# RWKV chunk products on 64x64 quarters of the array, gram matrices by 64-row halves, in a one-core Trainium2 decoder block

## The chip, the cores and the metric

One core of a Trainium2 chip runs one launch of a hybrid decoder block. The metric is the device time of a launch in microseconds. The kernel before takes 2877.19 us (median of 3 runs, 2877.06 to 2877.37).

The core has five engines, each with an instruction queue of its own that it works through in order: PE (TensorE, matmuls, with the loading of weights recorded apart as PEld), DVE (VectorE), ACT (ScalarE), POOL (GpSimd) and SP (which only issues transfers here). They wait for one another through semaphores.

## The reference

Input x is 512 tokens of 2048 channels. The block computes a fused projection of the normalised input, RWKV-7 time mixing (16 heads of 64), sliding-window attention, gated merging, and a gated convolutional FFN. The change lies in the time mixing alone:

```python
def step(state, inp):
    r_t, k_t, v_t, w_t, ka_t, kb_t = inp
    sa = jnp.einsum('bhvk,bhk->bhv', state, ka_t)
    state = (state * w_t[:, :, None, :] + sa[..., None] * kb_t[:, :, None, :]
             + v_t[..., None] * k_t[:, :, None, :])
    y = jnp.einsum('bhvk,bhk->bhv', state, r_t)
    return state, y
...
_, y = lax.scan(step, state0, xs)          # over 512 tokens, per head
mu = jnp.mean(y, axis=-1, keepdims=True)
var = jnp.mean(jnp.square(y - mu), axis=-1, keepdims=True)
y = ((y - mu) * lax.rsqrt(var + GN_EPS)).reshape(B, S, RW_DIM)
```

## The kernel before, in words

The scan is computed in 8 chunks of 64 tokens (`NCH`, `C`). Two heads are worked on together as a pair, head 0 on partitions 0 to 63 and head 1 on 64 to 127 (`HV`); there are 8 pairs. A pair goes through three functions. `early(p)` projects k, r and v and makes decays and keys. `late(p)` makes, for every chunk:

- the gram products (L700): `BKK` (keys times inverse decay, 128 columns: own head's b, other kind's k) against `BAR` (a and r of both heads, 256 columns), masked by DVE into `BX`, `OA`, `MD`, `MO` (L704). A 128x128 result holds a 64x64 block for each head and two blocks that belong to no head, masked to zero, so that a product over 128 rows serves both heads.
- the inverse of a triangular matrix by doubling: `tt`, `X`, `AI`, `BT` are set up (L708 to L720, with transposes of `BX` at L713), then five levels (`LEVELS[1:]`) of two f16 products each, `mm3(AI, ..)` and `mm3(BT, ..)` (L761, L762).
- the bulk products of all chunks: `GV` and `KV` (L724, from `OA` and `KO` with `VV`, the centred v).
- the chain over chunks: `psG` (L802) to `G` on DVE, `psU` (L808) to `UU` on ACT, `psS` (L815) to `SS` on DVE, and so to the next chunk.
- the output products y of a chunk: `MO` with `VV`, `MD` with `UU`, `BAR` with `SS` (L821, L822, L824), added up in one PSUM tile, copied to `yt`.

`final(p)` normalises `yt` into `yd`, transposes it (L843) and applies the gate (L609). After each pair three gate tiles of the big projection are computed (`emit_gate`). The calls go `late(p)`, `early(p + 1)`, `final(p)`, gates.

The projections in `early` and in the gates are three matmuls per 128 rows of weights, in a split-float form (L260 to L262, 512 columns). Their weights come by transfer as `raw`, and ACT and DVE split them into `whi` (L243) and `wlo` (L244), 12 matmuls for each split, 4 buffers deep. 288 of these matmuls fall between one pair's first gram product and the next pair's.

A scheduler at build time sets the order on each engine from its own estimates; `pin` ties an instruction behind the one traced before it on its engine. The order is then fixed. PSUM tiles named `bulk` come from a ring of 3 banks. `OA`, `KO` and `yd` share one buffer (tag "ko"), `GV` and `yt` another.

Of the kernel before, what the change touches and what calls it, by code (L numbers as in the profile page):

```python
# [8 lines left out]
F32 = mybir.dt.float32  # L9
# [125 lines left out]
def block_kernel(ctx: ExitStack, tc: tile.TileContext, d: Dims, a: dict, out: bass.AP):  # L135
# [145 lines left out]
    if True:  # L281
# [243 lines left out]
        with ExitStack() as pr:  # L525
# [142 lines left out]
            def late(p, st):  # L668
# [24 lines left out]

                BKE = wk.tile([P, NCH, P], F32, name="BKE", tag="BKE")
                dve.tensor_tensor(BKE, BKK, ee.unsqueeze(2).to_broadcast([P, NCH, P]), op=ALU.mult)
                OA = wk.tile([P, NCH, P], F32, name="OA", tag="ko")
                for n0 in range(0, NCH, 2):
                    ps = bulk()
                    for j in range(2):
                        pe.matmul(ps[:, j * 4 * C : (j + 1) * 4 * C], BKK[:, n0 + j],  # L700
                                  BAR[:, n0 + j].rearrange("p a h c -> p (a h c)"), start=True, stop=True)
                    pq = ps.rearrange("p (n a c) -> p n a c", n=2, a=2)
                    for t, a, nm in ((BX, 0, "own"), (OA, 0, "other"), (MD, 1, "own"), (MO, 1, "other")):
                        dve.tensor_tensor(t[:, n0 : n0 + 2], pq[:, :, a], mb(nm, 2)[:, :, a * P : (a + 1) * P], op=ALU.mult)  # L704
                for g in range(2):
                    ns = slice(g * HN, (g + 1) * HN)
                    for h, (lo, hi) in enumerate(HV):
                        dve.tensor_tensor(tt[lo:hi, ns], BX[lo:hi, ns, lo:hi], mb("m1", HN, (lo, hi)), op=ALU.mult)  # L708
                    dve.tensor_tensor(tt[:, ns], tt[:, ns], mb("istack", HN), op=ALU.add)
                    split(X[:, 0, ns], X[:, 1, ns], tt[:, ns])  # L710
                    ps = bulk().rearrange("p (n c) -> p n c", c=P)
                    for j in range(HN):
                        pe.transpose(ps[:, j], BX[:, g * HN + j], ident)  # L713
                    at_ = wk.tile([P, HN, P], F32, name="at_", tag="at_")
                    dve.scalar_tensor_tensor(at_, ps, SG, mb("idsg", HN), op0=ALU.mult, op1=ALU.add)
                    split(AI[:, 0, ns], AI[:, 1, ns], at_)
                    act.activation(BX[0:C, ns, 0:C], tt[0:C, ns], AF.Copy, scale=1.0 / SG)
                    dve.tensor_scalar(BX[C:P, ns, C:P], tt[C:P, ns], 1.0 / SG, None, op0=ALU.mult)
                    for i in range(2):
                        dve.tensor_tensor(BT[:, i, ns], AI[:, i, ns], mb("t1bd", HN), op=ALU.mult)  # L720
                def bulk_mm(dst, l, r):
                    ps = bulk()
                    for n in range(NCH):
                        pe.matmul(r3(ps)[:, n], l(n), r(n), start=True, stop=True)  # L724
                    act.activation(dst, r3(ps), AF.Copy)

                ps = bulk()
                for t in range(NT):
                    ts = slice(t * P, (t + 1) * P)
# [2 lines left out]
                dve.reduce_sum(vm, r3(ps), axis=AX.X)  # L732
                dve.tensor_scalar(vm, vm, -1.0 / HD, None, op0=ALU.mult)
                for a, (fl, fh) in enumerate(HV):
                    for h in range(2):
                        ol, oh = HV[1 - h]
                        dve.tensor_tensor(VV[ol:oh, a::2], r3(ps)[fl:fh, h::2],
                                          vm[fl:fh, h::2].unsqueeze(2).to_broadcast([C, NT, C]), op=ALU.add)
                GV = wk.tile([P, NCH, C], F32, name="GV", tag="yt")
                bulk_mm(GV, lambda n: OA[:, n], lambda n: VV[:, n])  # L740
                for g in range(2):
                    ns = slice(g * HN, (g + 1) * HN)
                    ps = bulk().rearrange("p (n c) -> p n c", c=P)
                    for j in range(HN):
                        pe.transpose(ps[:, j], BKE[:, g * HN + j], ident)
                    if g == 0:
                        KO = wk.tile([P, NCH, P], F32, name="KO", tag="ko")
                        pool.memset(KO[0:C, :, 0:C], 0.0)
                        pool.memset(KO[C:P, :, C:P], 0.0)
                    for h, (lo, hi) in enumerate(HV):  # L750
                        ol, oh = HV[1 - h]
                        act.activation(KD[lo:hi, ns, lo:hi], ps[lo:hi, :, lo:hi], AF.Copy)
                        act.activation(KO[lo:hi, ns, ol:oh], ps[lo:hi, :, ol:oh], AF.Copy)
# [45 lines left out]
                for n in range(NCH):  # L799
                    if n:  # L800
                        ps = chn.tile([P, C], F32, name="psG", tag="chn")
                        pe.matmul(ps, BAR[:, n, 0].rearrange("p h c -> p (h c)"), SS[:, n], start=True, stop=True)  # L802
                        G = wk.tile([P, C], F32, name="G", tag="G", bufs=2)
                        dve.tensor_tensor(G, GV[:, n], ps, op=ALU.add)
                    else:
                        G = GV[:, 0]
                    ps = chn.tile([P, C], F32, name="psU", tag="chn")
                    pe.matmul(ps, BX[:, n], G, start=True, stop=True)  # L808
                    act.activation(UU[:, n], ps, AF.Copy)
# [6 lines left out]
                    dve.tensor_tensor(SS[:, n + 1], KV[:, n], ps, op=ALU.add)  # L816

                ps = bulk()
                for n in range(NCH):
                    dst = r3(ps)[:, n]  # L820
                    pe.matmul(dst, MO[:, n], VV[:, n], start=True, stop=False)  # L821
                    pe.matmul(dst, MD[:, n], UU[:, n], start=False, stop=n == 0)  # L822
                    if n:
                        pe.matmul(dst, BAR[:, n, 1].rearrange("p h c -> p (h c)"), SS[:, n], start=False, stop=True)  # L824
                yt = wk.tile([P, NCH, C], F32, name="yt", tag="yt")
                act.activation(yt, r3(ps), AF.Copy)
                return ag, bon, yt

            def final(p, st):
                ag, bon, yt = st  # L830
                sq = wk.tile([P, NCH, C], F32, name="gn", tag="gn")
                act.activation(sq, yt, AF.Square)
                ss = wk.tile([P, NCH], F32, name="ssy", tag="ssy")
                dve.reduce_sum(ss, sq, axis=AX.X)
                rs = rsqrt_small(wk, ss, 1.0 / HD, GN_EPS)
                yd = wk.tile([P, NT, 2, C], F32, name="yd", tag="ko")
                for a, (al, ah) in enumerate(HV):
                    for h, (lo, hi) in enumerate(HV):
                        dve.tensor_tensor(yd[al:ah, :, h], yt[lo:hi, a::2],
                                          rs[lo:hi, a::2].unsqueeze(2).to_broadcast([C, NT, C]), op=ALU.mult)  # L840
                ps = bulk()
                for t in range(NT):
                    pe.transpose(ps[:, t * P : (t + 1) * P], yd[:, t].rearrange("p h c -> p (h c)"), ident)  # L843
# [607 lines left out]
```

## Time and profile before

| | |
|---|---|
| median of 3 runs | 2877.19 us |
| the profiled execution | 2876.5 us, span 2874.7 us |
| from the first gram product to the last pair's transposes | about 332 to 1139 us |
| one pair, gram to gram | 102.45 us |
| granted PE clock over the span | 0.996 |

The span is what the profile covers of the execution. In the profile an f32 matmul appears as two records, each with a weight load of its own, since it runs in two passes; the other kinds appear as one. A record's duration is its latency: records follow one another closer than that, so the cost of a matmul in a dense stretch is the distance from its start to the next start. `128*128` in a row is the size of the weights, and the two shapes behind it are those of what is streamed.

### The profile page before, as it was taken

How to read it: one execution, taken by the hardware profiler on the slowest of the kernel's cores; microseconds unless marked ns; L12 is line 12 of the kernel's file. 1: busy time of each engine (PE TensorE's matmuls, PEld its weight loads, DVE VectorE, ACT ScalarE, POOL GpSimd, SP SyncE). 2: the span in 40 equal slices, each digit the busy share in tenths (PEclk: the TensorE clock that was granted, in tenths of full speed). 3: DMA queues.
4: the chain of work that ended last, by engine and by line, in shares of the span. 5: the costliest groups of instructions: out<-in, count | busy, mean ns of one | idle time of the engine just before them, and what ended most of it. 6: DMA issues, size and time to landing. Idle time of an engine off the chain costs nothing.

```text
span 2874.7 us, 46847 instructions
## 1 busy us (share of the span) xinstructions
PE 2810.6 (98%) x17970; PEld 2455.0 (85%) x17970; DVE 1957.0 (68%) x3388; ACT 1323.9 (46%) x2191; POOL 235.1 (8%) x319
## 2 busy tenths in 40 slices
PE   7999999999999999999999899999999999999999
PEld 6888777777777777788888899999999999888887
DVE  5566666767776675345668787777778777655655
ACT  5345344435434434322456445455555545544444
POOL 0101000000000001111000010101011010000000
PEclk9999999999999999999999999999999999999999
DMA  6855666666656657878777788888888887877775
GB/s 199 228 158 148 182 163 168 160 161 153 166 144 162 174 152 183 269 237 272 258 262 209 211 237 229 222 233 244 230 226 226 242 236 217 315 246 241 258 254 190
DMA packets 223857, 608.35 MB, mean 212 GB/s; under 512 B 24577, under 2 KB 44689, under 8 KB 222609
## 3 DMA queue, kind: packets, MB, share of 16 engines
q1 hardware_dynamic: 156096, 432.86, 46.6%
q0 software_dynamic: 36832, 134.24, 24.2%
q10 hardware_dynamic: 30704, 38.27, 3.8%
q8 instruction: 141, 2.31, 0.3%
q14 instruction: 84, 0.68, 0.1%
HBM read 554.59 MB, written 174.40 MB: 254 GB/s over the span
## 4 chain that ended last, share of the span: by engine, by line
PE 59%; DMA 3%; DVE 2%; ACT 1%; issue 1%; ACTq 0%; SPq 0%; DVEq 0%
PE X L1152 17%; PE X L1019 10%; PE Y L1019 9%; PE Y L1152 8%; PE Z L1152 4%; PE acc L262 3%; PE acc L260 3%; PE acc L261 3%; DMA raw<-in_w_z_dram 1%; DMA raw<-in_w_dn_dram 1%; DMA raw<-in_w_b_dram 0%; DMA raw<-in_w_up_dram 0%; DVE wlo L1135 0%; PE ps_t L1083 0%; DMA gate_d<-gt 0%
## 5 line engine op out<-in xcount | busy, mean ns | idle before, releaser
L260 PE MATMUL acc<-xhi,whi 128*128 128x512 f32 x1120 | 454.0, 405 | 1.9 <-ACT whi L243 1.9
L262 PE MATMUL acc<-xhi,wlo 128*128 128x512 f32 x1120 | 449.4, 401 | 3.2 <-DVE wlo L244 3.2
L261 PE MATMUL acc<-xlo,whi 128*128 128x512 f32 x1120 | 452.1, 404 | 0.0
L243 ACT ACTIVATE whi<-raw 128x512 fp32r<-128x512 f32 x352 | 219.8, 629 | 468.1 <-PE acc L261 355.0
L244 DVE TENSOR_TENSOR wlo<-raw,whi 128x512 fp32r<-128x512 f32 x352 | 240.3, 689 | 233.0 <-ACT whi L243 214.8
L1012 DVE TENSOR_TENSOR wlo<-raw,whi 128x1024 fp32r<-128x1024 f32 x210 | 257.1, 1224 | 205.3 <-ACT whi L1011 205.3
L1011 ACT ACTIVATE whi<-raw 128x1024 fp32r<-128x1024 f32 x210 | 222.6, 1060 | 289.7 <-PE X L1019 147.8
L1152 PE MATMUL X<-b,whi 128*128 128x256 f32 x1472 | 270.4, 284 | 2.3 <-DVE u L1172 0.9
L1152 PE MATMUL X<-t,whi 128*128 128x256 f32 x1408 | 259.9, 285 | 9.9 <-DVE u L1172 9.4
L1135 DVE TENSOR_TENSOR wlo<-raw,whi 128x1024 fp32r<-128x1024 f32 x176 | 215.0, 1223 | 77.8 <-ACT whi L1134 77.7
L1152 PE MATMUL Y<-t,whi 128*128 128x256 f32 x1408 | 257.1, 283 | 0.0
L262 PEld LDWEIGHTS acc<-xhi,wlo 128*128 128x128 f32 x1120 | 211.2, 189 | 45.7 <-DVE wlo L244 8.2
L260 PEld LDWEIGHTS acc<-xhi,whi 128*128 128x128 f32 x1120 | 211.7, 189 | 38.3 <-ACT whi L243 3.2
L261 PEld LDWEIGHTS acc<-xlo,whi 128*128 128x128 f32 x1120 | 211.6, 189 | 38.1 <-issue 2.2
L1134 ACT ACTIVATE whi<-a 128x1024 fp32r<-128x1024 f32 x132 | 139.4, 1056 | 218.7 <-DVE a L1128 214.6
L1152 PEld LDWEIGHTS X<-b,whi 128*128 128x128 f32 x1472 | 230.7, 193 | 3.1 <-issue 2.4
L1152 PEld LDWEIGHTS X<-t,whi 128*128 128x128 f32 x1408 | 221.7, 194 | 10.4 <-DVE u L1172 6.8
L1152 PEld LDWEIGHTS Y<-t,whi 128*128 128x128 f32 x1408 | 219.6, 192 | 0.0
L1152 PE MATMUL X<-b,wlo 128*128 128x256 f32 x736 | 209.1, 284 | 2.1 <-DVE wlo L1135 2.1
L1135 DVE TENSOR_TENSOR wlo<-a,whi 128x1024 fp32r<-128x1024 f32 x132 | 161.7, 1225 | 69.8 <-ACT whi L1134 69.2
L1152 PE MATMUL X<-t,wlo 128*128 128x256 f32 x704 | 200.4, 285 | 0.0
L1152 PE MATMUL Y<-t,wlo 128*128 128x256 f32 x704 | 199.2, 283 | 0.0
(777 smaller groups left out, 5987.4 us busy)
## 6 DMA issues: line engine op xcount, KB each, us to landing
raw<-in_w_up_dram SPq DMA_DIRECT2D x180, 512.0 KB
raw<-in_w_z_dram SPq DMA_DIRECT2D x288, 256.0 KB
s_dn<-in_w_dn_dram POOLq DMA_DIRECT2D x88, 512.0 KB, 6.8
raw<-in_w_up_dram POOLq DMA_DIRECT2D x88, 512.0 KB, 8.7
raw<-s_dn SPq DMA_DIRECT2D x88, 512.0 KB
raw<-in_w_dn_dram SPq DMA_DIRECT2D x66, 512.0 KB
a<-in_w_up_dram SPq DMA_DIRECT2D x48, 512.0 KB
s_dn<-in_w_dn_dram SPq DMA_DIRECT2D x44, 512.0 KB
```

The lines of the kernel that those rows point to most:

```text
L243: pin(act.activation(hi, raw, AF.Copy))
L244: pin(dve.tensor_tensor(lo, raw, hi.bitcast(F32), op=ALU.subtract))
L260: pe.matmul(acc, whi[:, j], xhi[:, k], start=first, stop=False)
L261: pe.matmul(acc, whi[:, j], xlo[:, k], start=False, stop=False)
L262: pe.matmul(acc, wlo[:, j], xhi[:, k], start=False, stop=last)
L1011: act.activation(whi, wr, AF.Copy)
L1012: dve.tensor_tensor(wlo, wr, whi.bitcast(F32), op=ALU.subtract)
L1019: pe.matmul(dst, l[:, q, ts], r[:, es], start=fst and j == 0, stop=lst and j == 2, skip_group_check=True)
L1134: pin(act.activation(hi, t, AF.Copy))
L1135: pin(dve.tensor_tensor(lo, t, hi.bitcast(F32), op=ALU.subtract))
L1152: pin(pe.matmul(ps, l[:, k], r[:, k], start=start and k + i == 0, stop=last and i == 2, skip_group_check=True))
```

## The change

Four things change, all in the time mixing. (1) The bulk products `KV`, `GV` and y are issued head by head, each a 64x64 weight block on its own quarter of the array (`heads_mm`), pinned one behind another in unbroken bursts; `OA`, `MO`, `MD`, `KO` lose their zero blocks (`AM`, `OW`, dense `KO`). (2) The gram products are issued by halves of 64 rows, the two halves into two PSUM banks. (3) The setup of `tt`, `X`, `AI`, `BT` runs on dense blocks over all 8 chunks at once, with 4 transposes of two chunks in place of 8. (4) The y products move from `late(p)` to the start of `final(p)`, with the last chunk first.

```diff
-            MO, MD = (bd.tile([P, NCH, P], F32, name=n) for n in ("MO", "MD"))
+            OW, AM = (bd.tile([P, 2, NCH, C], F32, name=n) for n in ("OW", "AM"))
...
+            for t in (AI, BT):
+                pool.memset(t[0:C, :, :, C:P], 0.0)
+                pool.memset(t[C:P, :, :, 0:C], 0.0)
...
+            def heads_mm(dst, l, r, start, stop):
+                for h, (lo, hi) in reversed(list(enumerate(HV))):
+                    w = l[lo:hi] if l.shape[-1] == C else l[lo:hi, lo:hi]
+                    pin(pe.matmul(dst[lo:hi], w, r[lo:hi], start=start, stop=stop, skip_group_check=True))
+
+            def bulk_mm(dst, l, r):
+                ps = bulk()
+                for n in reversed(range(NCH)):
+                    heads_mm(r3(ps)[:, n], l(n), r(n), True, True)
+                act.activation(dst, r3(ps), AF.Copy)
...
-                for n0 in range(0, NCH, 2):
-                    ps = bulk()
-                    for j in range(2):
-                        pe.matmul(ps[:, j * 4 * C : (j + 1) * 4 * C], BKK[:, n0 + j],
-                                  BAR[:, n0 + j].rearrange("p a h c -> p (a h c)"), start=True, stop=True)
-                    pq = ps.rearrange("p (n a c) -> p n a c", n=2, a=2)
-                    for t, a, nm in ((BX, 0, "own"), (OA, 0, "other"), (MD, 1, "own"), (MO, 1, "other")):
-                        dve.tensor_tensor(t[:, n0 : n0 + 2], pq[:, :, a], mb(nm, 2)[:, :, a * P : (a + 1) * P], op=ALU.mult)
+                for n0 in range(0, NCH, HN):
+                    gram = [bulk().rearrange("p (n a c) -> p n a c", a=2, c=C) for _ in HV]
+                    for j in range(HN):
+                        for h, (lo, hi) in enumerate(HV):
+                            pin(pe.matmul(gram[h][:, j], BKK[lo:hi, n0 + j], BAR[lo:hi, n0 + j, :, h], start=True, stop=True))
+                    for t, nm in ((OW, "own"), (AM, "other")):
+                        for h, (lo, hi) in enumerate(HV):
+                            rs = HV[h if t is OW else 1 - h]
+                            dve.tensor_tensor(t[lo:hi, :, n0 : n0 + HN].rearrange("p a n c -> p n a c"), gram[h][slice(*rs)], causal(nm, rs, (lo, hi), HN), op=ALU.mult)
+                dve.tensor_tensor(tt, OW[:, 0], mb("m1", NCH), op=ALU.mult)
+                dve.tensor_tensor(tt, tt, mb("istack", NCH), op=ALU.add)
+                split(X[:, 0], X[:, 1], tt)
+                ps = bulk().rearrange("p (t c) -> p t c", c=P)
+                for t in range(NT):
+                    pe.transpose(ps[:, t], OW[:, 0, 2 * t : 2 * t + 2].rearrange("p n c -> p (n c)"), ident)
...
+                        dve.scalar_tensor_tensor(at_[lo:hi, a::2], ps[fl:fh, :, lo:hi], SG, mb("istack", NT, (fl, fh)),
+                                                 op0=ALU.mult, op1=ALU.add)
+                for lo, hi in HV:
+                    split(AI[lo:hi, 0, :, lo:hi], AI[lo:hi, 1, :, lo:hi], at_[lo:hi])
...
-                        KO = wk.tile([P, NCH, P], F32, name="KO", tag="ko")
-                        pool.memset(KO[0:C, :, 0:C], 0.0)
-                        pool.memset(KO[C:P, :, C:P], 0.0)
+                        KO = wk.tile([P, NCH, C], F32, name="KO", tag="ko")
...
+                GV = wk.tile([P, NCH, C], F32, name="GV", tag="yt")
                 bulk_mm(KV, lambda n: KO[:, n], lambda n: VV[:, n])
+                bulk_mm(GV, lambda n: AM[:, 0, n], lambda n: VV[:, n])
...
-                    pe.matmul(ps, BX[:, n], G, start=True, stop=True)
+                    pin(pe.matmul(ps, BX[:, n], G, start=True, stop=True))
...
+            def final(p, st):
+                ag, bon = st
                 ps = bulk()
-                for n in range(NCH):
+                for n in reversed(range(NCH)):
                     dst = r3(ps)[:, n]
-                    pe.matmul(dst, MO[:, n], VV[:, n], start=True, stop=False)
-                    pe.matmul(dst, MD[:, n], UU[:, n], start=False, stop=n == 0)
+                    heads_mm(dst, OW[:, 1, n], UU[:, n], True, False)
+                    heads_mm(dst, AM[:, 1, n], VV[:, n], False, n == 0)
                     if n:
-                        pe.matmul(dst, BAR[:, n, 1].rearrange("p h c -> p (h c)"), SS[:, n], start=False, stop=True)
+                        heads_mm(dst, BAR[:, n, 1].rearrange("p h c -> p (h c)"), SS[:, n], False, True)
```

On PE, where `KV` and `GV` stand in the third pair; before (L724 are the bulk products, L745 the transposes of `BKE`, L761 and L762 the first level):

```order
L262 MATMUL acc<-xhi,wlo 128x512
L724 MATMUL bulk<-VV,OA 128x64
L745 MATMUL bulk<-ident,BKE 128x128 x4
L260 MATMUL acc<-xhi,whi 128x512
L724 MATMUL bulk<-VV,OA 128x64 x7
L745 MATMUL bulk<-ident,BKE 128x128 x4
L261 MATMUL acc<-xlo,whi 128x512
```

and after (L617 are the quarter products, L772 the first level):

```order
L260 MATMUL acc<-xhi,whi 128x512
L261 MATMUL acc<-xlo,whi 128x512
L617 MATMUL bulk<-VV,KO 64x64 x16
L617 MATMUL bulk<-VV,AM 64x64 x16
L772 LDWEIGHTS AI
L772 MATMUL bulk<-XIW,AI 128x64
```

The two products are one burst now, straight ahead of the first level, and the transposes of `BKE` have moved ahead of it; from the first gram product to this burst 59 projection matmuls stand on PE, and then 12 between the first level's two products, where 14 stood.

On PE, the end of the chain in the third pair; before:

```order
L808 MATMUL psU<-G,BX 128x64
L262 MATMUL acc<-xhi,wlo 128x512
L260 MATMUL acc<-xhi,whi 128x512
L261 MATMUL acc<-xlo,whi 128x512
L262 MATMUL acc<-xhi,wlo 128x512
L822 MATMUL bulk<-UU,MD 128x64
L824 MATMUL bulk<-SS,BAR 128x64
L260 MATMUL acc<-xhi,whi 128x512
```

and after:

```order
L819 MATMUL psU<-G,BX 128x64
L261 MATMUL acc<-xlo,whi 128x512
L262 MATMUL acc<-xhi,wlo 128x512
L617 MATMUL bulk<-UU,OW 64x64 x2
L617 MATMUL bulk<-VV,AM 64x64 x2
L617 MATMUL bulk<-SS,BAR 64x64 x2
L617 MATMUL bulk<-UU,OW 64x64 x2
```

All 23 y products of the pair (46 quarter products) now stand here, with two projection matmuls between them and the last `psU`. Behind them 29 projection matmuls stand ahead of the transposes of `yd`, where 34 stood.

On DVE, the same place; before (L678 writes the r part of `BAR`, which the y products read; L834 is the first step of the normalisation):

```order
L677 SCALAR_TENSOR_TENSOR BAR<-kk,Et 64x8x64 x2
L244 TENSOR_TENSOR wlo<-raw,whi 128x512
L678 TENSOR_TENSOR BAR<-rz,Et 64x8x64 x2
L834 TENSOR_REDUCE ssy<-gn 128x8
L695 TENSOR_TENSOR BKE<-BKK,ee 128x1024
```

and after:

```order
L709 TENSOR_TENSOR BKE<-BKK,ee 128x1024
L827 TENSOR_TENSOR SS<-KV,psS 128x64
L244 TENSOR_TENSOR wlo<-raw,whi 128x512
L815 TENSOR_TENSOR G<-GV,psG 128x64
L691 SCALAR_TENSOR_TENSOR BAR<-kk,Et 64x8x64 x2
L692 TENSOR_TENSOR BAR<-rz,Et 64x8x64 x2
L244 TENSOR_TENSOR wlo<-raw,whi 128x512
L845 TENSOR_REDUCE ssy<-gn 128x8
```

`BKE` has moved into the chain, and a weight split now stands behind the `BAR` pieces.

More of the change, by code (lines that the diff above doesn't have):

```diff
@@ L705, in late @@
-                for g in range(2):
-                    ns = slice(g * HN, (g + 1) * HN)
-                    for h, (lo, hi) in enumerate(HV):
[L708 to L720, printed above, removed]
@@ L721, in bulk_mm, with causal @@
-                def bulk_mm(dst, l, r):
-                    ps = bulk()
-                    for n in range(NCH):
-                        pe.matmul(r3(ps)[:, n], l(n), r(n), start=True, stop=True)
-                    act.activation(dst, r3(ps), AF.Copy)
+                def causal(nm, rows, cols, n):
+                    m = K[nm].rearrange("p (a c) -> p a c", a=2)[slice(*rows), :, slice(*cols)]
+                    return m.unsqueeze(1).to_broadcast([C, n, 2, C])
+                for n0 in range(0, NCH, HN):
[7 more added lines that the diff above has]
+                            dve.tensor_tensor(t[lo:hi, :, n0 : n0 + HN].rearrange("p a n c -> p n a c"), gram[h][slice(*rs)], causal(nm, rs, (lo, hi), HN), op=ALU.mult)
@@ new lines, in late @@
+                dve.tensor_tensor(tt, OW[:, 0], mb("m1", NCH), op=ALU.mult)
[4 more added lines that the diff above has]
+                    pe.transpose(ps[:, t], OW[:, 0, 2 * t : 2 * t + 2].rearrange("p n c -> p (n c)"), ident)
+                at_ = wk.tile([P, NCH, C], F32, name="at_", tag="at_")
+                for a, (fl, fh) in enumerate(HV):
+                    for h, (lo, hi) in enumerate(HV):
+                        dve.scalar_tensor_tensor(at_[lo:hi, a::2], ps[fl:fh, :, lo:hi], SG, mb("istack", NT, (fl, fh)),
+                                                 op0=ALU.mult, op1=ALU.add)
@@ new lines, in late @@
+                for lo, hi in HV:
+                    split(AI[lo:hi, 0, :, lo:hi], AI[lo:hi, 1, :, lo:hi], at_[lo:hi])
+                act.activation(BX[0:C, :, 0:C], tt[0:C], AF.Copy, scale=1.0 / SG)
+                dve.tensor_scalar(BX[C:P, :, C:P], tt[C:P], 1.0 / SG, None, op0=ALU.mult)
+                for lo, hi in HV:
+                    m = K["t1bd"][lo:hi, lo:hi].unsqueeze(1).unsqueeze(1).to_broadcast([C, 2, NCH, C])
+                    dve.tensor_tensor(BT[lo:hi, :, :, lo:hi], AI[lo:hi, :, :, lo:hi], m, op=ALU.mult)
@@ L734, in late @@
                 for a, (fl, fh) in enumerate(HV):
-                    for h in range(2):
-                        ol, oh = HV[1 - h]
-                        dve.tensor_tensor(VV[ol:oh, a::2], r3(ps)[fl:fh, h::2],
+                    for h, (lo, hi) in enumerate(HV):
+                        dve.tensor_tensor(VV[lo:hi, a::2], r3(ps)[fl:fh, h::2],
                                           vm[fl:fh, h::2].unsqueeze(2).to_broadcast([C, NT, C]), op=ALU.add)
-                GV = wk.tile([P, NCH, C], F32, name="GV", tag="yt")
-                bulk_mm(GV, lambda n: OA[:, n], lambda n: VV[:, n])
                 for g in range(2):
@@ L816, in late @@
                     dve.tensor_tensor(SS[:, n + 1], KV[:, n], ps, op=ALU.add)
+                return ag, bon
+            def final(p, st):
+                ag, bon = st
                 ps = bulk()
-                for n in range(NCH):
+                for n in reversed(range(NCH)):
                     dst = r3(ps)[:, n]
-                    pe.matmul(dst, MO[:, n], VV[:, n], start=True, stop=False)
-                    pe.matmul(dst, MD[:, n], UU[:, n], start=False, stop=n == 0)
+                    heads_mm(dst, OW[:, 1, n], UU[:, n], True, False)
+                    heads_mm(dst, AM[:, 1, n], VV[:, n], False, n == 0)
                     if n:
-                        pe.matmul(dst, BAR[:, n, 1].rearrange("p h c -> p (h c)"), SS[:, n], start=False, stop=True)
+                        heads_mm(dst, BAR[:, n, 1].rearrange("p h c -> p (h c)"), SS[:, n], False, True)
                 yt = wk.tile([P, NCH, C], F32, name="yt", tag="yt")
                 act.activation(yt, r3(ps), AF.Copy)
-                return ag, bon, yt
-            def final(p, st):
-                ag, bon, yt = st
                 sq = wk.tile([P, NCH, C], F32, name="gn", tag="gn")
```

3 lines of the change are left out of this document (1 added, 2 removed).

## The prediction

> **What bounds the kernel now.** I read the engines' shares first, then busy time per stretch, then the groups of the stage that the change touches, then the order of events in one pair of heads.
>
> ```profile
> PE 2810.6 (98%) x17970; PEld 2455.0 (85%) x17970; DVE 1957.0 (68%) x3388; ACT 1323.9 (46%) x2191; POOL 235.1 (8%) x319
> 436.19:538.63 102.44, 100.33 (x662) 80.13 (x661) 72.64 (x178) 44.38 (x96) 8.11 (x11) 1.00 0.65 161
> 538.63:641.08 102.45, 100.37 (x662) 80.14 (x661) 72.63 (x178) 44.35 (x96) 8.12 (x11) 1.00 0.63 159
> ```
>
> TensorE (PE) is busy 98% of the span. The second and third rows run from the first gram product of one pair to that of the next (length, then busy time of PE, weight load, DVE, ACT, POOL, then granted clock, DMA share, GB/s): every pair takes 102.45 us and repeats the last one, so I price one pair and take it 8 times. PE is in order and always has projection matmuls in between, so what it saves is a gain unless it then waits for DVE or ACT. The groups that the change touches, all 8 pairs:
>
> ```profile
> L700 PE MATMUL bulk<-BAR,BKK 128*128 128x256 f32 x128 | 30.9, 383 | 0.4 <-DVE bon L664 0.4
> L821 PE MATMUL bulk<-VV,MO 128*128 128x64 f32 x128 | 25.0, 277 | 0.0
> L822 PE MATMUL bulk<-UU,MD 128*128 128x64 f32 x128 | 24.3, 271 | 0.0
> L824 PE MATMUL bulk<-SS,BAR 128*128 128x64 f32 x112 | 21.7, 275 | 0.0
> L724 PE MATMUL bulk<-VV,KO 128*128 128x64 f32 x128 | 17.3, 278 | 0.4
> L724 PE MATMUL bulk<-VV,OA 128*128 128x64 f32 x128 | 16.1, 269 | 0.0
> L713 PE MATMUL bulk<-ident,BX 128*128 128x128 f32 x64 | 10.9, 272 | 0.0
> ```
>
> A pair has 8 gram products but 16 records: an f32 matmul is recorded twice, as two passes. The duration is latency; what a record costs is the distance to the next start, which the order of events gives (the second figure is the length of the merged run):
>
> ```profile
> 538.63 2.75 PE L700 MATMUL bulk<-BAR,BKK 128*128 128x256 f32 x12
> 543.07 0.60 PE L713 MATMUL bulk<-ident,BX 128*128 128x128 f32 x4
> 557.25 1.67 PE L724 MATMUL bulk<-VV,OA 128*128 128x64 f32 x14
> 595.86 0.19 PE L761 MATMUL bulk<-XIW,BT 128*128 128x64 f16 x1
> 595.88 0.18 PE L762 MATMUL bulk<-XIW,BT 128*128 128x32 f16 x1
> 595.91 0.19 PE L761 MATMUL bulk<-XIW,BT 128*128 128x64 f16 x1
> 596.22 1.00 PE L374 MATMUL bulk<-cst,lg 128*128 128x2 f32 x8
> 597.85 0.40 PE L262 MATMUL acc<-xhi,wlo 128*128 128x512 f32 x1
> 598.09 0.39 PE L260 MATMUL acc<-xhi,whi 128*128 128x512 f32 x1
> ...
> 72.54 0.08 PEld L377 LDWEIGHTS mi<-ident,rq 128*8 128x8 f32 x1 [0.36 <-DVE rq L197]
> 72.54 0.19 PEld L262 LDWEIGHTS acc<-xhi,wlo 128*128 128x128 f32 x1
> 72.65 0.19 PEld L260 LDWEIGHTS acc<-xhi,whi 128*128 128x128 f32 x1
> ```
>
> Distances: L700 (2.75-0.38)/11 = 0.215 us; L724 (1.67-0.28)/13 = 0.107; L374 (1.00-0.25)/7 = 0.107; transposes (0.60-0.27)/3 = 0.11; f16 about 0.027; a projection matmul 0.23. L374 streams 2 columns and L724 64 at the same 0.107, so neither is paced by its stream but by loading 128 columns of weights twice. L700 streams 256 columns, and there the stream sets 0.215, which makes 0.054 for 64 columns. The weight rows show that the load goes by columns: the load behind L377's 8 columns starts at the same hundredth, the one behind 128 columns 0.11 later. So a 64-column load is estimated at 0.054.
>
> **The change, part by part, for one pair.**
>
> *Bulk products on quarters.* Now (16+16+16+16+14) = 78 records at 0.107 = 8.3 us. After it, each product is one 64x64 matmul per head: 156 records. Bounds for their distance: 0.107 if narrow weights bought nothing (16.7 us), 0.027 if two heads, which share no row and no output column of the array, run beside each other and only the start rate of the f16 rows is left (4.2 us). One head alone would need 0.054 of load and 0.054 of stream, one hidden behind the other: 156 x 0.054 = 8.4 us, nothing gained. I take 0.028, since load and stream of one half leave the other half idle and the f16 rows show that PE can start that often: 4.4 us.
>
> [...]
>
> *Gram products by halves.* Now 16 x 0.215 = 3.44 us. After it 32 records of 128 columns streamed and 128 loaded: 0.107 each if serial (3.4 us), 0.054 if the halves overlap (1.7 us), which I take for the same reason. *First transposes:* 4 fewer, -0.44 us.
>
> *Entering and leaving the small tiles.* Four bursts (two gram, KV with GV, y), 8 switches. The rows above, f16 to f32 to projection, show no loss, but all use the whole array: 0 below. Above, the pipeline empties: a record's 0.275 less its 0.107 = 0.17 us. I take 0.08, the middle: 0.6 us.
>
> *DVE behind the gram.* This stretch decides how much of the above counts.
>
> ```profile
> 517.91 1.38 DVE L677 SCALAR_TENSOR_TENSOR BAR<-kk,Et 64x512 f32<-64x512 f32 x2
> 539.87 0.42 DVE L704 TENSOR_TENSOR BX<-bulk,cst 128x256 f32<-128x256 f32 x1
> 544.85 0.41 DVE L704 TENSOR_TENSOR MO<-bulk,cst 128x256 f32<-128x256 f32 x1
> 545.18 0.84 DVE L708 TENSOR_TENSOR tt<-BX,cst 64x256 f32<-64x256 f32 x2
> 548.70 1.29 DVE L720 TENSOR_TENSOR BT<-AI,cst 128x512 f16<-128x512 f16 x2
> 554.61 0.69 DVE L244 TENSOR_TENSOR wlo<-raw,whi 128x512 fp32r<-128x512 f32 x1
> 555.33 1.75 DVE L737 TENSOR_TENSOR VV<-bulk,vm 64x256 f32<-64x256 f32 x4
> ...
> 555.35 0.50 PE L262 MATMUL acc<-xhi,wlo 128*128 128x512 f32 x1 [0.28 <-DVE wlo L244]
> 562.85 0.48 PE L260 MATMUL acc<-xhi,whi 128*128 128x512 f32 x1
> ...
> L748 POOL MEMSET KO<- x8: 517/520/520, 354.0 to 1071.4; 64x512 f32 x8
> PEld bulk L724 <- POOL KO L749: 3.6, 8, 0.5
> ```
>
> From 539.87, 1.24 us after the first gram product, to VV at 557.08 DVE works without a pause, 17.2 us, and PE already waits there for a weight split. The 16 gram evictions are 5.3 us of it. The new stretch: 8 evictions of 64x512 at 0.69 (as L677) = 5.5; tt twice and X's low part 2.0; four pieces of at_ at 0.44 (as VV) 1.75; two pieces of AI and BX 1.9; BT in two pieces of twice L720's length 2.5; the sum vm 0.7; two weight splits, one more than now, 1.35; VV 1.75: 17.4. So VV stands at 1.2 + 17.4 = 18.6 us after the first gram product, as now (18.45), and the burst of KV and GV can't end before it. PE reaches the burst at 59 projection matmuls x 0.23 = 13.6, 16 transposes 1.8, gram 1.7, switches 0.3: 17.4, and waits 1.2. The gram's gain is thus lost to DVE. Stretch from gram to the end of the first level's f16 products: now 538.63 to 562.85 = 24.2; after it 18.6 + 64 x 0.028 + 0.2 + 0.43 = 21.0. That is -3.2 us; it holds POOL's clearing of KO, which goes and cost PE 3.6/8 = 0.45. It ends with one projection matmul fewer than now and the first level then has 12 to cover it in place of 14: +0.2 for the one, +0.3 for the wait.
>
> POOL's four new clearings of AI and BT stand once ahead of the first pair, where POOL is 8% busy; by L748's 0.52 (half as long per partition) they would cost 4 x 1.0 us if nothing hid them. I take 0. KO's and GV's copies on ACT keep their sizes.
>
> *The y products, moved behind the chain.*
>
> ```profile
> 518.32 0.33 PE L808 MATMUL psU<-G,BX 128*128 128x64 f32 x2
> 519.05 0.20 ACT L809 ACTIVATE UU<-psU 128x64 f32<-128x64 f32 x1
> 519.64 0.39 PE L824 MATMUL bulk<-SS,BAR 128*128 128x64 f32 x2
> 522.09 1.22 DVE L695 TENSOR_TENSOR BKE<-BKK,ee 128x1024 f32<-128x1024 f32 x1
> 528.47 0.66 PE L843 MATMUL bulk<-ident,yd 128*128 128x128 f32 x4 [0.63 <-DVE yd L839]
> ```
>
> 46 of the 78 records become 92: 4.9 to 2.6 us, with two switches -2.15. They filled the chain's waits; projection matmuls, three where two stood, now do. The burst starts with chunk 7, which needs UU at 519.25, 0.93 after psU's start, with two projection matmuls (0.6 with psU itself) ahead: +0.25. Behind the last y product yd comes 8.6 us later with 34 projection matmuls (7.8) as cover. Now 29 (6.7). But BKE (1.22) leaves that stretch of DVE, while both BAR pieces (1.38, as L677) wait for the whole burst: about 7.5 needed, wait 0.8 as now; +0.1.
>
> **Sum** for a pair: -3.2 + 0.2 + 0.3 - 2.15 + 0.25 + 0.1 = -4.5 us; 8 pairs -36. The profiled execution took 2876.5 us (span 2874.7), 0.7 below the median 2877.19; against the median: 2841 us.
>
> **The rivals.**
>
> *Not all of it arrives.* A DVE or ACT wait comes back at the levels or at yd, or each switch empties and refills the array. Emptying plus refilling at 0.17 each makes 8 x 0.34 = 2.7 in place of 0.6, so -2.4 a pair: 2858 us. For it: PE already waits at four places of a pair, and no row shows a switch. [...]
>
> *No overlap of the two heads.* 0.054 a record, gram 0.107: PE then comes to the burst at 19.1, after VV, and the stretch takes 19.1 + 3.5 + 0.6 = 23.2; y +0.45. Sum -1.0 + 0.5 + 0.45 + 0.1 = about 0: 2877, no change. For it: the trace has no two matmuls side by side. With emptying as well (+2.1): 2894.
>
> *Slower: narrow weights cost as much as wide ones.* At 0.107 a record the bulk products take 16.7 for 8.3: +8.4 a pair, 2945 us. The price is 156 records, the saving 4.5 at 0.028, so it turns at 0.028 + 4.5/156 = 0.057. Against it: L377's load.
>
> **How the numbers follow.** The forecast has 0.58; its own range is 2830 (VV not binding: another 1.2 a pair) to 2853 (every switch at 0.17 and the waits twice as long). Partly returned 0.14, no overlap 0.17, no overlap and emptying 0.05, wide price 0.06. No change means within 0.2%, 5.8 us, about what a measurement of this kernel can tell. Faster: 0.58 + 0.14 + 0.02 of no overlap = 0.74; same 0.12; slower 0.03 + 0.05 + 0.06 = 0.14. A range of 2829 to 2881 leaves out the 0.11 of the two slow cases and the ends of the others.
>
> **What would show it.** Right: records of the 64x64 products 0.025 to 0.035 apart, gram records about 0.055, a pair of 98 us, PE waiting at the KV burst for VV, DVE busy from the gram to VV as long as now. Wrong: 0.054 apart (no overlap), a gap of 0.2 or more at each end of a burst (emptying), or a wait of more than 2 us ahead of yd or the f16 products. If PE waits for VV by more than 2 us, my DVE pieces are too cheap.

## The result, and the profile after

The changed kernel takes 2844.28 us (median of 4 runs, 2843.01 to 2852.0). The kernel before, on the same chip, takes 2877.28 (2877.06 to 2880.6). The ratio is 0.9888, with a 95% interval of 0.9869 to 0.9908: faster by 1.1%. The forecast was 2841, in a range of 2829 to 2881. Right were the sign, the size and the main mechanism; the working has one price that was about half of the true one (switches), a gram term that leaves out the products without a neighbour, and a reading of VectorE's role that does not hold beyond its own stage.

The engines' shares, and the two stretches from gram product to gram product that follow 531.60, of the profile after (2843.21 us, span 2841.4):

```profile
PE 2778.1 (98%) x18690; PEld 2411.2 (85%) x18690; DVE 1952.9 (69%) x3276; ACT 1324.4 (47%) x2175; POOL 230.8 (8%) x307
531.60:630.65 99.05, 96.55 (x752) 74.57 (x752) 71.94 (x164) 44.26 (x94) 6.77 (x9) 1.00 0.66 165
630.65:729.68 99.03, 96.57 (x752) 74.58 (x751) 71.91 (x164) 44.23 (x94) 7.09 (x10) 1.00 0.66 165
```

A pair now takes 99.05 us, 3.4 less than before; 4.5 were forecast. The work of VectorE (DVE, third busy time) is almost unchanged at 71.9 us. What fell is PE's: 3.8 us of its busy time. PE's order of events from the gram products to the first level, then around y:

```profile
531.60 1.38 PE L718 MATMUL bulk<-BAR,BKK 64*128 64x128 f32 x18
532.91 0.50 PE L260 MATMUL acc<-xhi,whi 128*128 128x512 f32 x1
...
535.03 1.13 PE L718 MATMUL bulk<-BAR,BKK 64*128 64x128 f32 x14
536.09 0.44 PE L728 MATMUL bulk<-ident,OW 128*128 128x128 f32 x2
...
541.27 0.66 PE L756 MATMUL bulk<-ident,BKE 128*128 128x128 f32 x4 [0.25 <-ACT KO L762]
...
550.87 1.15 PE L617 MATMUL bulk<-VV,KO 64*64 64x64 f32 x32
551.82 1.13 PE L617 MATMUL bulk<-VV,AM 64*64 64x64 f32 x32
552.88 0.20 PE L772 MATMUL bulk<-XIW,AI 128*128 128x64 f16 x1
...
613.18 0.28 PE L617 MATMUL bulk<-VV,AM 64*64 64x64 f32 x4
613.29 0.28 PE L617 MATMUL bulk<-SS,BAR 64*64 64x64 f32 x4
...
615.63 0.28 PE L617 MATMUL bulk<-VV,AM 64*64 64x64 f32 x4
615.84 0.50 PE L260 MATMUL acc<-xhi,whi 128*128 128x512 f32 x1
```

A row x4 is one chunk's product, two heads with two records each. From 613.18 to 615.63 there are 21 of them in 2.45 us: 0.117 us each, 0.029 a record. The KV and GV burst is 64 records in 2.01 us. The 18 gram records take 1.31 us, 0.073 each on average, but that holds the ends of the burst. By the starts of the single records, two of them, one of each half, start every 0.112 us inside the burst, so 0.056 each; the ninth product has no neighbour and takes 0.112 a record, and the 0.2 us that are left go into entering and leaving. The 14 records behind 535.03 are seven products in the same way. A new wait stands at 541.27: BKE's second transposes wait for a bank that ACT empties into `KO`.

To see where a pair's 3.4 us come from, I charged every PE record with the time to the next start (less recorded waits) and took the mean of five pairs from 538.63 and 531.60 on:

| us in a pair | before | after |
|---|---|---|
| KV, GV and y products | 8.47 | 4.83 |
| gram products | 3.13 | 2.36 |
| first transposes | 0.63 | 0.33 |
| chain products | 3.94 | 3.74 |
| 288 projection matmuls, with the delays that stretch them | 71.47 | 72.46 |
| waits recorded ahead of a record | 2.10 | 2.52 |
| all else | 12.72 | 12.82 |
| sum | 102.46 | 99.06 |

So 4.9 us of work went, and 1.4 us came back as longer distances between projection matmuls and as waits. PE's waits from 330 to 1110 us, before and then after (us, times, longest):

```profile
PE bulk L761 <- DVE XIW L207: 5.0, 16, 0.3
PE bulk L843 <- DVE yd L839: 4.5, 7, 0.6
PE bulk L761 <- ACT whi L243: 4.3, 16, 0.4
```

```profile
PE bulk L772 <- ACT whi L243: 5.9, 18, 0.4
PE bulk L772 <- DVE XIW L207: 5.6, 18, 0.5
PE bulk L854 <- DVE yd L850: 4.3, 7, 0.6
PE bulk L756 <- ACT KO L762: 1.9, 8, 0.3
```

The first two rows of after are the second products of the levels, those with `BT`, L761 before (both products of a level issue from L761 and L762): 11.5 us where it was 9.3. The yd wait stayed, the `KO` wait is new.

The whole run gained more than seven or eight pairs give. From the first gram product to the last pair's transposes 27 us went (332.09 to 1138.78 before, 331.63 to 1111.40 after), and 6 more behind them. A part of these stands in PE's waits on the split weights just behind the pairs (1138 to 1375 us before, 1111 to 1342 after):

```profile
PE acc L260 <- ACT whi L243: 1.9, 2, 1.7
```

```profile
PE acc L260 <- ACT whi L243: 0.3, 1, 0.3
```

No experiment was made on that part.

### The profile page after: what moved, and what is told of

It reads as the page before. It is cut to its first block, busy times and chain, and to the rows that moved or that the text cites. A ratio compares the mean times of both kernels' runs of the same rounds, so it can differ in the third digit from the quotient of the medians.

```text
span 2841.4 us, 48140 instructions
## 1 busy us (share of the span) xinstructions
PE 2778.1 (98%) x18690; PEld 2411.2 (85%) x18690; DVE 1952.9 (69%) x3276; ACT 1324.4 (47%) x2175; POOL 230.8 (8%) x307
## 4 chain that ended last, share of the span: by engine, by line
PE 61%; DVE 2%; DMA 1%; ACT 1%; issue 1%; ACTq 0%; SPq 0%; DVEq 0%; POOLq 0%
PE X L1163 17%; PE X L1030 11%; PE Y L1030 9%; PE Y L1163 8%; PE Z L1163 4%; PE acc L262 3%; PE acc L260 3%; PE acc L261 3%; DMA raw<-in_w_z_dram 1%; DMA raw<-in_w_up_dram 1%; DVE wlo L1146 0%; DMA s_dn<-s_dn 0%; PE bulk L617 0%; ACT whi L1145 0%; PE ps_t L1094 0%
```

## The experiments

All start from the changed kernel but one, and change the time mixing alone. Times are medians, ratios are to the kernel before in the same session (0.9888 for the change itself). A pair's length is the distance between first gram products, the median of seven, and steadier than the time: runs of one kernel differ by up to 12 us.

| kernel | time, us | ratio, 95% interval | pair, us |
|---|---|---|---|
| changed kernel | 2844.3 | 0.9869 to 0.9908 | 99.10 |
| head by head | 2873.4 | 0.9988 to 1.0011 | 102.79 |
| gram by half | 2863.2 | 0.9951 to 0.9977 | 101.63 |
| many switches | 2980.7 | 1.0349 to 1.0384 | 115.97 |
| few switches | 2890.0 | 1.0040 to 1.0070 | 104.97 |
| y ascending | 2855.5 | 0.9907 to 0.9937 | 100.30 |
| half of BT on POOL | 2851.1 | 0.9898 to 0.9927 | 100.00 |
| BKE early | 2856.5 | 0.9913 to 0.9954 | 101.59 |
| VV late | 2854.6 | 0.9905 to 0.9935 | 100.01 |
| KV and GV alone | 2873.7 | 0.9985 to 1.0004 | 102.63 |
| gram on quarters | 2848.4 | 0.9884 to 0.9920 | 99.17 |
| even chunks first | 2851.0 | 0.9891 to 0.9944 | 100.47 |
| the last two together | 2856.2 | 0.9904 to 0.9950 | 101.01 |

**Head by head.** Do quarters gain by their narrow weights or by their neighbours?

```diff
-for n in reversed(range(NCH)):
-    heads_mm(r3(ps)[:, n], l(n), r(n), True, True)
+for hv in reversed(HV):
+    for n in reversed(range(NCH)):
+        heads_mm(r3(ps)[:, n], l(n), r(n), True, True, (hv,))
```

> The same quarter products in KV, GV and y, but all chunks of one head ahead of all of the other's, so that neighbours (but one pair a burst) stand on the same quarter. The changed kernel takes 2844 us with 156 quarter records a pair at 0.029 to 0.031 us. Theory (neighbours on different quarters run at once): without such neighbours a record takes twice that, 0.055 to 0.060; the KV and GV burst goes from 2.0 to 3.5 us, the y burst from 2.8 to 5.2, a pair from 99.05 to about 103, the whole to 2870 to 2880 us. Rival (a quarter's 64-column weights are cheap by themselves, order does not matter): records stay at 0.03 and the time at 2844.

Its y burst, where a row is now one head's product of one chunk, and a pair:

```profile
629.05 0.28 PE L617 MATMUL bulk<-SS,BAR 64*64 64x64 f32 x2
629.17 0.28 PE L617 MATMUL bulk<-UU,OW 64*64 64x64 f32 x2
629.29 0.28 PE L617 MATMUL bulk<-VV,AM 64*64 64x64 f32 x2
545.74:648.53 102.79, 100.35 (x753) 78.37 (x752) 71.86 (x164) 44.49 (x94) 7.29 (x10) 1.00 0.62 159
```

One head takes the 0.117 us that both heads took: 0.058 a record. All engines but PE have the same order as in the changed kernel, and the pair gets 3.7 us longer, the whole gain. The rival falls: narrow weights halve a record (0.107 to 0.058) while there are twice as many, and the gain of these products is all in the overlap of neighbours on different quarters. Two such neighbours start 0.01 us apart (at 611.02 and 611.03 below under y ascending), and such a pair takes 0.058 us.

**Gram by half.** Within each group of eight products the half changes twice in place of seven times: 4 changes a pair for 14 (the count in the expectation is off).

```diff
-for j in range(HN):
-    for h, (lo, hi) in enumerate(HV):
+for h, j in ((1, 0), (1, 1), (1, 2), (0, 0), (0, 1), (0, 2), (0, 3), (1, 3)):
```

> In each group of four chunks the gram products run three of the upper half, four of the lower, one of the upper, in place of halves in turn (6 changes of half fewer of 14 a pair's 16 products have; the rest of the order shifts a little with it). Theory (halves in turn run beside each other, 0.073 us a record): products without a neighbour on the other half take 0.107, the 32 records go from 2.4 to about 3.2 us; if the stage is held by PE, a pair gets 0.8 us longer (time 2850); if VectorE holds it, as the prediction had it, the pair stays within 0.3 us (2844 to 2847). Rival (0.073 is what 128 moving columns take on any half): records stay at 0.073 and the time at 2844.

```profile
641.39 2.04 PE L718 MATMUL bulk<-BAR,BKK 64*128 64x128 f32 x22
645.15 1.13 PE L718 MATMUL bulk<-BAR,BKK 64*128 64x128 f32 x10
```

The gram takes 3.03 us in place of 2.36 by the distances, so the overlap of halves is real. VV comes 0.5 us later (19.63 us after the first gram product). The total is worse than either theory said: the scheduler placed the rest differently, and from 330 to 1110 us PE waits 9.6 us for SS ahead of the chain's psG and 3.9 us for VV, two waits that the changed kernel does not have. Together they are about the pair's other 1.8 us, seven times, which are thus not the gram's price.

**Many and few switches.** The price of going between quarters and the whole array.

```diff
+def full_mm(n):
+    pin(pe.matmul(chn.tile([P, C], F32, name="psD", tag="chn"), ident, VV[:, n], start=True, stop=True))
 ...
 for n in reversed(range(NCH)):
     heads_mm(r3(ps)[:, n], l(n), r(n), True, True)
+    full_mm(n)          # many; few: a loop of its own behind this one
```

> After each chunk of the KV, GV and y bursts stands one added dense product of 128 rows and 128 columns on 64 moving columns (24 a pair, never read), so that the array goes between quarters and the whole 42 times a pair more often than in the next kernel, which has the same 24 products at the ends of the bursts. By the theory of the prediction (0.08 us a switch) this kernel is 42 x 8 x 0.08 = 27 us slower than the next one; if a switch empties and refills the array (0.34 us) it is 114 us slower; if a switch costs nothing the two agree within 3 us. The products themselves (0.22 us each, 5.2 us a pair) add some 41 us to both, for 2885 us without switches, 2912 with 0.08.

> The 24 added dense products a pair as in the kernel before, but eight in a row at the end of each burst: 0.22 us each, so 5.2 us a pair and about 2885 us, with the bursts' own records unchanged at 0.029 to 0.031 us.

Many switches, in its KV burst, then later in the GV burst, and busy times (PE first) with the granted clock (third figure from the end) over the beginning of the KV burst, over what follows it, and over the y burst:

```profile
588.12 0.33 PE L617 MATMUL bulk<-VV,KO 64*64 64x64 f32 x4
588.38 0.43 PE L620 MATMUL psD<-VV,ident 128*128 128x64 f32 x2
588.75 0.33 PE L617 MATMUL bulk<-VV,KO 64*64 64x64 f32 x4
...
595.61 0.48 PE L617 MATMUL bulk<-VV,AM 64*64 64x64 f32 x4
596.02 0.69 PE L620 MATMUL psD<-VV,ident 128*128 128x64 f32 x2
596.64 0.48 PE L617 MATMUL bulk<-VV,AM 64*64 64x64 f32 x4
...
587.50:590.80 3.30, 3.30 (x34) 2.63 (x34) 2.23 (x4) 1.19 (x2) 0.24 (x1) 1.00 0.80 281
591.50:601.50 10.00, 10.00 (x61) 7.76 (x61) 0.00 (x0) 0.83 (x2) 0.81 (x1) 0.50 0.65 133
662.80:669.40 6.60, 6.60 (x109) 5.59 (x109) 1.00 (x3) 0.12 (x1) 0.81 (x1) 1.00 0.50 128
```

At full clock a chunk and its dense product take 0.63 us where the two need 0.117 + 0.215 = 0.33, so two switches cost 0.30: 0.15 each. In the y burst, with three chunk products ahead of each dense one, a period of 0.86 us gives (0.86 - 0.57) / 2 = 0.15 as well. But after some 3.5 us at this pace the granted clock falls to 0.50, and a period takes 1.03. So of the 91 us between the two kernels 42 x 8 x 0.15 = 50 us are switches, and the lower clock costs the other 40. An estimate bears this out: the clock stands at 0.50 for 13.7 us of a pair (590.9 to 604.5 in this one), and with 0.63 us of work in each 1.03 that loses 5 us a pair. The few-switches kernel itself took 5.9 us a pair: 24 x 0.215 = 5.2, two switches more, and waits.

**y ascending.** What is the closed burst worth? `pin` alone does not close it: without it in `heads_mm` every engine's order, as built, is the same. What closes the y burst is that chunk 7 comes first and needs the last `UU`.

```diff
-for n in reversed(range(NCH)):
+for n in range(NCH):
     dst = r3(ps)[:, n]
```

> The y products in ascending order of chunk (in the changed kernel the last chunk, which needs the last UU, is first, so nothing of the burst can start before the chain ends). The first chunks' products are then issued between the steps of the chain, as the dense ones were before the change: 12.9 changes between quarters and the whole array a pair in place of 4.1. At 0.15 us a change (the pair of changes around an added product costs 0.30 us at full clock in the kernel with many switches) a pair gets 1.3 us longer, less at most 0.1 of the wait for UU: some 10 us, 2853 to 2855. By the prediction's 0.08 it is 2849; if the closed burst is worth nothing, 2843 or below.

```profile
609.13 0.28 PE L617 MATMUL bulk<-UU,OW 64*64 64x64 f32 x4
609.34 0.43 PE L826 MATMUL psS<-UU,KD 128*128 128x64 f32 x2
609.71 0.33 PE L617 MATMUL bulk<-VV,AM 64*64 64x64 f32 x4
...
611.02 0.27 PE L617 MATMUL bulk<-VV,AM 64*64 64x64 f32 x1
611.03 0.27 PE L617 MATMUL bulk<-SS,BAR 64*64 64x64 f32 x1
```

From 609.13 to 609.71 a chunk product and a chain product take 0.58, 0.25 over their own 0.33, and the four records from 609.71 on take 0.05 longer than inside a burst: 0.30 for two switches, as above. A pair has ten switches more (14 for 4; the last pair has no more than before, whence the mean of 12.9 in the expectation) and is 1.2 us longer, 0.12 for each. The closed burst is worth some 8 to 10 us of the 33 (1.2 x 7 by the pairs, 0.9922 against 0.9888 by the ratios).

**Does VectorE set the stage from the gram to the first level, and is that stage worth shortening?** In the changed kernel VV is whole 19.12 us after the first gram product and the burst starts at 19.27. Four kernels, each meant to take one cause away.

*Half of BT on POOL:*

```diff
-for lo, hi in HV:
-    dve.tensor_tensor(BT[lo:hi, ...
+for eng, (lo, hi) in zip((pool, dve), HV):
+    eng.tensor_tensor(BT[lo:hi, ...
```

> One of BT's two products (64 partitions, 1024 elements, 1.24 us on VectorE) goes to POOL, which is idle there; the same values. In the changed kernel VectorE is busy almost without a break from the first gram product until VV is whole, 19.1 us after it, and the KV and GV burst starts 0.15 us after that. Theory (VectorE sets this stage): VV is whole about 1.2 us earlier (17.9), the burst starts at 18.0 to 18.4, and a pair falls by what PE waits there and no more, 0.5 to 0.9 us (4 to 7 us in all: 2837 to 2840), fewer projection matmuls standing ahead of the burst. Rival (PE's own work sets it): the burst stays at 19.2 and the time at 2844. Slower if POOL's product is late for the products that read BT, 12 us after it can start.

POOL, DVE, PE, and PE's waits:

```profile
550.02 2.56 POOL L740 TENSOR_TENSOR BT<-AI,cst 64x1024 f16<-64x1024 f16 x1 [10.01 <-DVE AI L207]
551.32 2.35 DVE L740 TENSOR_TENSOR BT<-AI,cst 64x1024 f16<-64x1024 f16 x1
556.25 1.15 PE L617 MATMUL bulk<-VV,KO 64*64 64x64 f32 x32 [1.23 <-DVE VV L750]
PE bulk L617 <- DVE VV L750: 9.8, 8, 1.2
```

VV is whole at 18.39, 0.73 earlier and not 1.2, since DVE's own half takes 2.35 us beside POOL's, where both halves took 2.47 on DVE alone. The burst follows VV at 18.54: VectorE does set it. Yet the pair is 0.9 us longer. The scheduler puts 51 projection matmuls ahead of the burst in place of 59, PE waits 1.2 us there, and the 8 stand elsewhere. Counted as in the table of a pair, PE's waits are 3.3 us in place of 2.5, which is nearly the whole loss.

*BKE early* (the whole block of BKE's transposes and copies stands ahead of the gram loop):

> The transposes of BKE and their eight copies on ScalarE stand ahead of the gram products in place of behind the transposes of vz, so that PE no longer waits there 0.4 us for a bank that ScalarE empties (KO). Theory (VectorE sets this stage): VV is still whole at 19.1 us and the burst at 19.3 us after the first gram product; PE only fills the time with other work, a pair falls by 0 to 0.4 us, and the time is 2841 to 2845. Rival (that wait is why the gain was smaller than predicted): the burst comes 0.4 us or more earlier in its stage, and the pair falls by 0.4 (2840 to 2841).

The `KO` wait is gone from its place, but 64 projection matmuls now stand ahead of the burst, which starts at 21.2, and PE waits 10.2 us in all for VV there (six times 1.7). Both theories had the pair too short. Part of the loss is the clock's: behind four of the six waits the granted clock falls to 0.50 for 3.4 us. Busy times ahead of one such fall, and in it:

```profile
452.70:456.10 3.40, 1.62 (x26) 1.01 (x27) 3.30 (x9) 0.52 (x2) 0.00 (x0) 1.00 0.00 0
456.20:459.50 3.30, 3.30 (x62) 3.18 (x59) 2.00 (x4) 1.56 (x4) 0.00 (x0) 0.50 0.36 104
```

These four pairs take 101.6 to 101.8 us, the two whose wait is followed by no fall 100.2. The gram products also stand in three bursts a pair now, not two, which makes two switches more.

*VV late* (the block from vz's transposes to `bulk_mm(GV, ..)` stands behind the first level):

> vz's transposes, VV, BKE's transposes and the KV and GV bursts stand behind the first level of the f16 products, since only the chain needs them: VectorE's 2.4 us for VV and its reduce no longer stand ahead of the first level. Theory (VectorE sets the stage up to the first level, and the waits of the levels are for lack of PE work beside them): the first level starts about 17 us after the first gram product in place of 21.3, the burst covers a wait behind it, and a pair falls by 0.5 to 1.5 us: 2832 to 2840. Rival: VectorE is as busy in the levels, so that VV and its reduce delay a later level by as much as they free here, and the time is 2842 to 2850.

The first level starts 11.15 us after the first gram product, 10 us earlier. The pair is 0.9 longer: PE now waits for XIW ahead of its transposes, for KO and for G (4.9, 4.4 and 2.5 us in all), and two projection matmuls stand inside its KV burst, two switches more a pair. The rival is right in size, 2854.6 a little over it, but the two largest of these waits are for ACT, not for VectorE.

*Even chunks first:*

```diff
+for a in range(2):
+    for ps, l in ((pk, KO), (pg, AM[:, 0])):
+        for n in reversed(range(a, NCH, 2)):
+            heads_mm(r3(ps)[:, n], l[:, n], VV[:, n], True, True)
```

> The KV and GV bursts in the order of VV's pieces: both products' even chunks, whose VV is written first, then both products' odd chunks; two banks held for both. The burst can start when half of VV is there, 0.86 us earlier: at 18.4 us after the first gram product in place of 19.3, with 33 projection matmuls ahead of it in place of 37. Theory (PE's work sets the pair, waits aside): only the 0.2 us that PE waits right ahead of the burst can be won, 0 to 0.2 us a pair, 2842 to 2846. Rival (the stage's length is on the path): the whole 0.86 us a pair, 2837.

The burst starts at 18.38, as expected, and the first level 0.9 us earlier. The pair is 1.4 us longer, with this wait, absent in the changed kernel:

```profile
PE psG L818 <- DVE SS L832: 8.2, 6, 3.9
```

So in all four the aimed wait or stage got shorter, and the pair longer. The pairs are those of one profiled execution each; by the whole time only BKE early lies clear of the changed kernel's interval. The 288 projection matmuls of a pair stay the same in number, but those ahead of the burst go from 59 to 51, 64, 34 (ahead of the first level) and 55: the scheduler deals them out anew, some to places that need no cover, and another place is short of them. That this dealing is the cause is read from these counts and from where the new waits stand; no kernel held the order fixed while VectorE got faster, and in BKE early and VV late the clock and the added switches have a share. In any case a stage's length was not a price here.

**KV and GV alone.** The kernel before with only these products on quarters in closed bursts.

```diff
-for n in range(NCH):
-    pe.matmul(r3(ps)[:, n], l(n), r(n), start=True, stop=True)
+for n in reversed(range(NCH)):
+    for h in (1, 0):
+        (lo, hi), rs = HV[h], slice(*HV[1 - h])
+        pin(pe.matmul(r3(ps)[lo:hi, n], l(n)[rs, lo:hi], r(n)[rs], ..., skip_group_check=True))
```

> The kernel before with one part of the change: KV and GV on quarters in closed bursts, last chunk first; y, the gram products and the setup as before. Theory: the 32 dense records of KV and GV (3.5 us) become 64 quarter records of 0.030 (1.9 us) and four changes of 0.15 (two bursts, apart here), so PE has 1.0 us a pair less; the burst waits for all of VV, which the first chunks of before did not (17.8 against 18.5 us after the first gram product); a pair goes from 102.45 to 101.3 to 101.8, the whole to 2866 to 2871. Rival (PE's work is all that counts and a change costs nothing): 1.6 us a pair, 2863. Rival (the stage is VectorE's and the gain is lost in it): 2873 to 2877.

```profile
537.38:639.98 102.60, 100.11 (x694) 78.90 (x693) 72.73 (x178) 44.30 (x96) 8.33 (x11) 1.00 0.60 158
PE bulk L845 <- DVE yd L841: 6.2, 7, 0.9
```

No gain. The two products went from 3.52 to 2.41 us of PE by the distances, but the burst starts at 18.56 in place of 17.76, since chunk 7 needs the last piece of VV, and the yd wait grew from 4.5 to 6.2. Counted as in the table of a pair, 0.7 us came back as longer distances between projection matmuls and 0.4 as waits. The third case of the expectation is right: this part's gain is lost without the others. What the y part, the gram and the setup give apart was not run.

**Gram on quarters, and both.** The only change of order is in the gram rows.

```diff
-pin(pe.matmul(gram[h][:, j], BKK[lo:hi, n0 + j], BAR[lo:hi, n0 + j, :, h], ...))
+for h, c in ((0, 0), (1, 1), (0, 1), (1, 0)):
+    (lo, hi), cs = HV[h], slice(*HV[c])
+    pin(pe.matmul(gram[h][cs, j], BKK[lo:hi, n0 + j, cs], BAR[lo:hi, n0 + j, :, h], ...))
```

> The gram products as 64x64 weight blocks on all four quarters in turn, two heads in two banks as now: 64 records a pair in place of 32 of 0.073 us; no other instruction moves on any engine. If a record's time goes by the columns of its weights (0.107 us for 128 columns on the whole array, 0.055 for 64 on one quarter, half of that with a neighbour elsewhere), it takes 0.027 to 0.030 and the gram 1.8 us in place of 2.36; VectorE, which waits for the first group and 0.4 us for the second, then starts earlier and VV is whole 0.2 to 0.5 us earlier (18.6 to 18.9 in place of 19.1); a pair falls by 0.2 to 0.5 us, the time to 2840 to 2842. Rival (the 128 moving columns set it): 0.036 or more a record, no change of the gram, of VV or of the time; 0.053 or more would make a pair 1 us longer (2852).

```profile
534.47 1.30 PE L719 MATMUL bulk<-BAR,BKK 64*64 64x128 f32 x34
537.87 1.10 PE L719 MATMUL bulk<-BAR,BKK 64*64 64x128 f32 x30
```

64 records take 2.26 us, 0.035 each on average: half the weight columns, twice the records, nearly the same time, as the rival said. But why is not shown. Inside the burst four records start every 0.109 us (0.027 each) where two started every 0.112, and by the shapes in the rows each quarter streams 128 columns in that time, as each half did, while a half still loads 128 columns of weights in all, so both rules give the same. The theory's saving came from setting 0.027 against the mean of 0.073, which holds the ends of the bursts. VV is 0.1 us later, the pair as before.

> The two kernels before together (gram on four quarters, even chunks first). By the theory the sum of both, 0.2 to 0.7 us a pair: 2838 to 2842. If neither moves a pair, 2844.

2856.2 and 101.01: neither expectation; it has the waits of even chunks first and gains nothing. None of these kernels is shown to beat the changed one.

## Why the prediction was right, and where not

- *Quarter records at 0.028:* right, 0.029 to 0.033, and by the mechanism named: with neighbours on the same quarter they take 0.058, near the 0.054 of the no-overlap rival, which gave 2877 and measured 2873.4. The wide price (0.107) did not occur.
- *y products, -2.15:* right. Their own work went from 4.95 to 2.83 us.
- *Switches, 0.08 each:* mis-sized, 0.15. For the four of the two quarter bursts that is 0.3 us a pair more; those of the gram were not measured apart. The rival with 0.34 each was too dear. The lower bound of 0 was misread: in the kernel before, a projection matmul behind an f32 product takes 0.31 (597.08 to 597.39, behind the row of L374) where they follow at 0.23.
- *Gram at 0.054 a record:* right where the halves stand side by side (0.056), but the term is mis-sized: 2.37 us and not 1.7. Groups of nine and of seven products leave one in each without a neighbour, 0.2 us more in all, and some 0.35 are the four switches, for which the prediction had 0.3 in its other term. The prediction called the gram's gain "lost to DVE" in any case, but DVE starts on the gram's results and waits 0.41 us for the second group:

```profile
532.79 1.39 DVE L722 TENSOR_TENSOR OW<-bulk,cst 64x512 f32<-64x512 f32 x2
...
536.01 1.41 DVE L722 TENSOR_TENSOR OW<-bulk,cst 64x512 f32<-64x512 f32 x2 [0.41 <-PE bulk L718]
...
549.00 1.72 DVE L750 TENSOR_TENSOR VV<-bulk,vm 64x256 f32<-64x256 f32 x4
```

- *VV at 18.6, a PE wait of 1.2 us for it:* VV at 19.1. PE came late itself, by the gram, by the `KO` wait and by a weight split, and hardly waits there. The stage, from the gram to the end of the first level's first f16 products, took 21.7 us in place of 21.0: -2.5 against before, where -3.2 was forecast.
- *POOL's clearing of `KO`, -0.45:* it went, but a wait for ACT's copies of `KO` took its place (1.9 us in eight), which the prediction did not have.
- *First level +0.3, yd as before:* the waits at the levels' second products rose by 2.2 us from 330 to 1110 us, in which the levels of eight pairs lie (0.3 a pair), and yd's stayed at 0.6. *UU wait +0.25:* smaller. The last projection matmul ahead of the y burst takes 0.32 (612.69 to 613.01) where they follow at 0.23, so about 0.1 with the entry.
- *The sum:* -4.5 a pair forecast, -3.4 measured; 2841 against 2844, since 6 us came from behind the pairs, where the sum had nothing. Of the 1.1 us a pair that are missing 0.7 are the stage's. So the time is closer than its working, and that is luck.

The prediction's step that does not carry is to read the stage's end as the gain ("This stretch decides how much of the above counts"). KV and GV alone end their stage 0.25 us earlier and gain nothing; half of BT on POOL, VV late and even chunks first end or begin it 0.7 to 10 us earlier and lose. What explains the 27 us of the pairs is that PE, at 98%, lost 4.9 us of work a pair while only 1.4 came back as waits and longer distances.

## What to carry to other kernels

- Two small products gained here from quarters when their instructions alternated between quarters and several followed one another (0.029 us a record, where neighbours on one quarter took 0.058); narrow blocks alone gained nothing. A switch between quarters and the whole array cost 0.15 us and the closed y burst was worth some 8 to 10 us; it takes a look at the order to know what closes a burst.
- Where one engine is full and its filler work is spread by a scheduler, count the work taken off that engine, then the waits that return. Shortening the other engines' part of a stage moved the filler, and the pair got longer each time.

## What the runs showed of the hardware that I had not expected

- A switch between quarters and the whole array cost 0.15 us at full clock (many switches: 0.63 us less 0.33 is 0.30 for two; 0.12 each over a whole pair under y ascending). That is less than half of the 0.34 of the prediction's rival.
- With switches so dense that products fill 0.33 of 0.63 us (many switches), the granted clock fell to 0.50 after about 3.5 us, although PE has a record at every moment ahead of the fall (3.30 of 3.30 us busy; a record's length is latency). At 0.57 of 0.86 it stayed at 1.00 over 6.60 us. In BKE early it fell to 0.50 behind 3.40 us with 1.62 of records. What makes it fall no run shows.
- A product of DVE took 2.35 us beside one of POOL (half of BT on POOL), for 1.24 in the changed kernel (2.47 for two). POOL's ends at 552.58, 1.26 us after DVE's start, and DVE's at 553.67, 1.09 us later. What delays DVE no run shows.
